# Six held float32 runs per head pair on TensorE, and PSUM banks filled with scores before their first read, in a two-layer attention and mLSTM kernel

## The chip, the cores and the metric

The kernel runs on one core of one Trainium2 chip. The metric is the device time of one execution in microseconds; of several executions the median counts. A profiled execution gives the trace: of each instruction its engine, start and length, and of the TensorE clock the granted share.

The engines are named as in the profile: PE is TensorE (PEld its weight loads), DVE is VectorE, ACT is ScalarE, POOL is GpSimd, SP is SyncE, which issues the weight transfers here. Each engine works off its own list of instructions in order and waits at an instruction until what it needs has been signalled.

## The reference

A sequence of 512 tokens of width 1024, all in float32, runs through two layers: dilated attention with a SwiGLU network, then an mLSTM mixer with a SwiGLU network, and a last norm. The change lies in the attention mixer:

```python
def dilated_attention_mixer(xn, positions, w_in, w_out):
    proj = (xn @ w_in).reshape(B, S, N_GROUPS, 3, ATTN_HEADS, ATTN_HEAD_DIM)   # 3 groups; q, k, v; 8 heads of 128
    for g, (window, dilation) in enumerate(((128, 1), (512, 4), (2048, 16))):
        q = apply_partial_rope(proj[:, :, g, 0], positions) * scale
        k = apply_partial_rope(proj[:, :, g, 1], positions)
        v = proj[:, :, g, 2]
        o, lse = dilated_window_attention(q, k, v, window, dilation)  # banded softmax attention in blocks of 128
        outs.append(o); lses.append(lse)
    wts = softmax(stack(lses), axis=0)              # the three groups are weighed by their log-sum-exp
    return einsum('gbsh,gbshd->bshd', wts, stack(outs)).reshape(B, S, ATTN_WIDTH) @ w_out
```

Its result is added to the input (h = h + mixer), and the first SwiGLU network follows.

## The kernel before

**Projections.** All large products are made in a split form: a float32 matrix is cut into a high and a low part in the type fp32r, and three of the four products of parts are added up (`SPLITS`, three matmuls for each 128 rows). `project` (matmuls in `multiply`, L206) makes one q, one k or group 0's v for two heads: 128 columns of weights stand in the array, the 512 tokens stream through, so its matmuls are 512 wide. `project_tokens` (L237) makes v of groups 1 and 2 with tokens as rows, in matmuls 256 wide. Each is worked off in two weight chunks of 512 rows; a chunk comes by one DMA on SP, ACT makes its high part (L175) and DVE its low part (L176). A chunk has 24 matmuls for each of two PSUM banks. These banks carry the tag "acc", of which there are three.

**Head pairs.** `attention_pair(pr)` runs four times, for two heads each (tiles a0... to a3...). It projects q and k of group 0, 1 and 2 (a1g0q, a1g0k, a1g1q ...), then v of the three groups. Beside these the attention itself is computed in plain float32 matmuls, which the trace shows as two passes each (a transpose as one):

- `scores(g, i, q, k)`: for head i of the pair the scores of a group. Group 0 has two banks with one matmul 128 and three 256 wide (L446), groups 1 and 2 one bank each with four matmuls 128 wide (L459). Behind each matmul DVE reads its part of the bank, adds the mask and takes the row's maximum in one instruction (L448, L460).
- `exponentials(o, i)`: DVE makes the bias `nb`, ACT the exponentials and their sums (L473, L479).
- `turn(i)`: v of group 0, projected with tokens as columns, is transposed (vT, L248) and copied by ACT (L604).
- `weigh()`: group 0 holds its tokens in another order than groups 1 and 2, so their maxima and sums change places by a matmul with a permutation (`exchange`, twice, xps, L492). DVE then makes the coefficients, with an Exp on ACT (L511), and scales the exponentials (L522, L525).
- `transposes(i)`: 15 blocks of exponentials of one head are transposed into four banks (pT, L248), which ACT copies out (pTs, L535).
- `values(i)`: 15 matmuls of these with v add up one head's output (L547, L552), which ACT copies to `o_heads` (oT, L554).

**Order.** The program's text is an order of its own: after each weight chunk `advance()` moves a tick forward and runs the steps that `defer(n, fn)` has put n ticks ahead. `S_AT` and `JOIN_AT` hold these distances. Tile's scheduler then places the instructions of each engine, beginning with those that are ready first by its own account; it may move matmuls of a step in between the projection's matmuls. PSUM has eight banks: three "acc", two "s" (scores, vT, pT), two "o" (values) and one "t" (exchange and small sums).

After the last pair `run_deferred()` runs what is left, the eight heads are split for the output projection (ao tiles, L190 and L191), and `out_project` multiplies with `attn_w_out` (awo0 to awo3). Norm, SwiGLU (f0j, fo), mLSTM and the second SwiGLU follow.

Of the kernel before, what the change touches and what calls it, by code (L numbers as in the profile page):

```python
# [11 lines left out]
F32 = mybir.dt.float32  # L12
# [22 lines left out]
PT_BUFS = 4  # L35
S_AT = ((2, 2), (2, 2), (2, 2))
JOIN_AT = ((5, 6, 7, 7, 8), (4, 6, 6, 6, 7))
STACK_AT = (9, 11, 14, 16)
# [32 lines left out]
def tile_hybrid_dilated_attn_mlstm(  # L71
# [67 lines left out]
    def run_deferred(due=lambda t: True):  # L139
        while True:  # L140
# [4 lines left out]
            ready[0][2]()  # L145

    def acc_tile(name):
        return ps.tile([P, 512], F32, tag="acc", name=name, bufs=3)
# [62 lines left out]
    def project(pairs, w2d, c0, nk, evac, name, hook=None, ready=()):  # L211

        acc = [acc_tile("%s_%d" % (name, m)) for m in range(2)]
        for ch in range((nk + 3) // 4):
            n = min(4, nk - 4 * ch)
            whl = ready[ch] if ready else split_chunk(weight_chunk(w2d, ch, c0, n, "%s_k%d" % (name, ch)))
            for m in range(2):
                multiply(acc[m], whl, pairs, ch, m, nk)
                if 4 * ch + n == nk and hook is None:
                    evac(m, acc[m])  # L220
            if 4 * ch + n == nk and hook is not None:
                hook()
                for m in range(2):
                    evac(m, acc[m])
            advance()

    def project_tokens(pairs, w2d, c0, evac, name, tok=lambda t, tb: t[:, tb * P:(tb + 1) * P]):

        acc = [acc_tile("%s_%d" % (name, m)) for m in range(2)]
        for ch in range(KC // 4):  # L230
            whl = split_chunk(weight_chunk(w2d, ch, c0, 4, "%s_k%d" % (name, ch)))
            for m in range(2):
                for i in range(2):
                    for k in range(4):
                        kk = ch * 4 + k
# [52 lines left out]
    with ExitStack() as actx:  # L288
# [138 lines left out]
        def attention_pair(pr):  # L427
# [7 lines left out]

            def scores(g, i, q, k):
                if g == 0:
                    p0[i] = ap.tile([P, 7, P], F32, tag="p0", name="%sp0_%d" % (nm, i), bufs=2)
                    for b2 in range(2):
                        sp = ps.tile([P, 512], F32, tag="s", name="%ss0" % nm, bufs=2)  # L440
                        o = 0
                        for b in (2 * b2, 2 * b2 + 1):
                            lo_ = max(b - 1, 0) * P
                            w = (b + 1) * P - lo_
                            pb = max(2 * b - 1, 0)
                            nc.tensor.matmul(sp[:, o:o + w], q[:, i, b * P:(b + 1) * P],  # L446
                                             k[:, i, lo_:lo_ + w], start=True, stop=True)
                            nc.vector.tensor_tensor_reduce(  # L448
                                p0[i][:, pb:pb + w // P, :].rearrange("p a b -> p (a b)"),
                                sp[:, o:o + w], mask_band[:, 2 * P - w:], 1.0, -3e38,  # L450
                                op0=ALU.add, op1=ALU.max, accum_out=own[:, 0, 0, i, b:b + 1])
                            o += w
                else:
                    if g == 1:
                        p12[i] = ap.tile([P, 8, P], F32, tag="p12", name="%sp12_%d" % (nm, i), bufs=2)
                    sp = ps.tile([P, 512], F32, tag="s", name="%ss%d" % (nm, g), bufs=2)
                    for c in range(4):
                        sl = slice(c * P, (c + 1) * P)
                        nc.tensor.matmul(sp[:, sl], q[:, i, sl], k[:, i, sl], start=True, stop=True)  # L459
                        nc.vector.tensor_tensor_reduce(  # L460
                            p12[i][:, 4 * (g - 1) + c, :], sp[:, sl], mask_causal if g == 1 else mask_dil,
                            1.0, -3e38, op0=ALU.add, op1=ALU.max, accum_out=mx[:, g - 1, i, c:c + 1])

# [18 lines left out]

            def exchange(o):

                ex = ap.tile([P, 2, 2, 4, 4], F32, tag="ex", name=nm + "ex", bufs=2)
                for st in range(2):
                    nc.vector.tensor_tensor(
                        ex[:, st].rearrange("p i b c -> p (i b) c"),
                        own[:, st, o].rearrange("p i b -> p (i b)").unsqueeze(2).to_broadcast([P, 8, 4]),
                        mask_part.unsqueeze(1).to_broadcast([P, 8, 4]), op=ALU.mult)  # L490
                xps = ps.tile([P, 512], F32, tag="t", name=nm + "xps", bufs=1)
                nc.tensor.matmul(xps[:, :64], perm, ex.rearrange("p s i b c -> p (s i b c)"), start=True, stop=True)  # L492
                ex2 = ap.tile([P, 4, 4, 4], F32, tag="ex2", name=nm + "ex2", bufs=2)
                nc.vector.tensor_tensor(
                    ex2, xps[:, :64].rearrange("p (s b c) -> p s c b", b=4, c=4),
                    mask_part.unsqueeze(1).unsqueeze(1).to_broadcast([P, 4, 4, 4]), op=ALU.mult)
                nc.vector.tensor_reduce(
                    oth[:, :, 1 - o], ex2.rearrange("p (s i) c b -> p s i c b", s=2), axis=AX.X, op=ALU.add)

            def weigh():  # L500

                exchange(0)
                exchange(1)
                cf = ap.tile([P, 16], F32, tag="cf", name=nm + "cf", bufs=2)
# [13 lines left out]
                for i in range(2):  # L518
# [4 lines left out]
                    for c in range(4):  # L523
                        blk = p12[i].rearrange("p (g c) k -> p c g k", g=2)[:, c]
                        nc.vector.tensor_scalar(blk, blk, cf4[:, 1, i, c:c + 1], None, op0=ALU.mult)  # L525

            def transposes(i):
                pts[i] = []
                for src, n0, n1 in ((p0[i], 0, 4), (p0[i], 4, 7), (p12[i], 0, 4), (p12[i], 4, 8)):
                    tp = ps.tile([P, 512], F32, tag="s", name=nm + "pT", bufs=2)  # L530
                    for j in range(n0, n1):
# [6 lines left out]
            def values(i):  # L538
                pt = pts[i]
                hs = slice(i * P, (i + 1) * P)  # L540
                op = ps.tile([P, 512], F32, tag="o", name=nm + "o", bufs=2)
                first = True
# [11 lines left out]
                nc.scalar.activation(o_heads[2 * pr + i], op, AF.Copy)  # L554

            for g in range(3):
                base = g * 3 * D + pr * 256
                qk = []
                for part in range(2):
                    t = tok_tile("%sg%d_%s" % (nm, g, "qk"[part]))  # L560
# [13 lines left out]
                    qk.append(t)  # L574
                for i in range(2):
                    at = S_AT[g][i]
                    defer(at, lambda g=g, i=i, qk=qk: scores(g, i, *qk))
                    if g != 1:
                        defer(at, lambda g=g, i=i: exponentials(g // 2, i))
            steps = (weigh, lambda: transposes(0), lambda: values(0), lambda: transposes(1), lambda: values(1))  # L580
            for at, fn in zip(JOIN_AT[pr == HEADS // 2 - 1], steps):
                defer(at, fn)
            for g in range(3):
# [8 lines left out]
                if g == 0:  # L592

                    vf = ap.tile([P, 2, SEQ], F32, tag="vf", name=nm + "vf")

                    def evac_f(m, acc, vf=vf):
                        nc.scalar.activation(in_order(vf[:, m]), by_block(acc), AF.Copy)

                    def turn(i, v=v, vf=vf):
                        tp = ps.tile([P, 512], F32, tag="s", name=nm + "vT", bufs=2)  # L600
                        for b in range(TB):
                            transpose_into(tp, b, vf[:, i, b * P:(b + 1) * P])
                        for b in range(TB):
                            nc.scalar.activation(v[:, b, i * P:(i + 1) * P], tp[:, b * P:(b + 1) * P], AF.Copy,  # L604
                                                 scale=rnat[:, b:b + 1])
                    project(pair, w_in, 2 * D + pr * 256, KC, evac_f, nm + "g0v")
                    for i in range(2):
                        defer(1, lambda i=i: turn(i))
                else:
                    project_tokens(pair, w_in, g * 3 * D + 2 * D + pr * 256, evac_v, "%sg%dv" % (nm, g))  # L610
# [4 lines left out]
        for k in range(HEADS - 2):  # L615
            split_act(pair[0][k], pair[1][k], o_heads[k], None)
        run_deferred()
        for k in range(HEADS - 2, HEADS):
            split_act(pair[0][k], pair[1][k], o_heads[k], None)

    def add_to_h(c):
        def evac(m, acc):
            nc.vector.tensor_tensor(h[2 * c + m], acc, h[2 * c + m], op=ALU.add)
        return evac

    def out_project(pairs, w2d, nk, name):
        for c in range(KC // 2):
            project(pairs, w2d, c * 256, nk, add_to_h(c), "%s%d" % (name, c))

    out_project(pair, attn_w_out[0], KC, "awo")  # L630

# [456 lines left out]
```

## Time and profile before

| What | Value |
|---|---|
| Runs | 1488.49, 1486.65, 1488.44 us; median 1488.44 |
| Profiled execution | 1486.96 us; its span 1485.2 us |
| Granted TensorE clock, mean | 0.999 |
| Attention pairs, first scores of one to first scores of the next | 47.67, 165.95, 284.25, 402.54 us: 118.3 us each |
| End of the last pair's values | 489.21 us |
| ACT and DVE busy in 166 to 284 us | 40.24 and 65.30 us of 118 |

The span reaches from the first to the last instruction of the engines; 1.76 us of the profiled execution lie around it. The ends of matmuls in the trace are modelled, and matmuls overlap in the pipe, so the distance from one start to the next says more than a record's length.

### The profile page before, as it was taken

The page shows a single profiled execution, that of the slowest core. Times are in us where ns is not written, and L with a number is a line of the kernel's source. Part 1 is how long each engine was busy: PE and PEld are TensorE (multiplying, and loading weights), DVE is VectorE, ACT ScalarE, POOL GpSimd, SP SyncE. Part 2 cuts the span into 40 slices and gives each one's busy share as a digit, 9 for nine tenths or more (in the row PEclk, how much of TensorE's full clock was granted, in tenths as well). Part 3 has the DMA queues.
Part 4 walks back from the last instruction along what each step waited for, and adds up shares of the span by engine and source line. Part 5 has one row for each costly group of instructions (what it writes and reads, how often), then busy time and mean ns, then how long its engine had stood idle before and what let it go on. Part 6 is the DMA issues. An engine that isn't in the chain of part 4 may idle for free. (4 is left out here: it accounts for less than half of the span.)

```text
span 1485.2 us, 18912 instructions
## 1 busy us (share of the span) xinstructions
PE 1468.7 (99%) x7492; PEld 1250.2 (84%) x7492; DVE 768.8 (52%) x1519; ACT 545.6 (37%) x997; POOL 102.8 (7%) x94
## 2 busy tenths in 40 slices
PE   7999999999999999999999999999999999999998
PEld 6889889889889888888888889798888888888887
DVE  7744653664565364444343338987755443443233
ACT  5343225225226342232232223785543332233223
POOL 1000000000000001110110000000000111110011
PEclk9999999999999999999999999999999999999999
DMA  6322222232232223333322333231232333323231
GB/s 191 100 72 86 85 86 71 72 100 78 65 96 71 82 94 100 100 89 97 99 93 93 106 92 87 59 100 58 67 118 87 98 99 100 99 88 98 85 99 72
DMA packets 127529, 134.71 MB, mean 91 GB/s; under 512 B 5392, under 2 KB 119376, under 8 KB 127440
## 3 DMA queue, kind: packets, MB, share of 16 engines
q1 hardware_dynamic: 125328, 131.55, 28.9%
q10 hardware_dynamic: 1808, 1.38, 0.3%
q8 instruction: 59, 0.97, 0.3%
q0 software_dynamic: 304, 0.56, 0.1%
q14 instruction: 30, 0.25, 0.1%
HBM read 131.38 MB, written 2.10 MB: 90 GB/s over the span
## 5 line engine op out<-in xcount | busy, mean ns | idle before, releaser
L206 PE MATMUL f1j<-n_h,f1j_h 128*128 128x512 f32 x352 | 137.1, 389 | 0.0
L206 PE MATMUL f0j<-n_h,f0j_h 128*128 128x512 f32 x352 | 137.1, 389 | 0.0
L206 PE MATMUL f0j<-n_h,f0j_l 128*128 128x512 f32 x352 | 137.0, 389 | 0.0
L206 PE MATMUL f1j<-n_h,f1j_l 128*128 128x512 f32 x352 | 137.0, 389 | 0.0
L206 PE MATMUL f0j<-n_l,f0j_h 128*128 128x512 f32 x352 | 136.9, 389 | 0.0
L206 PE MATMUL f1j<-n_l,f1j_h 128*128 128x512 f32 x352 | 136.9, 389 | 0.0
L176 DVE TENSOR_TENSOR f1j_l<-f1j_w,f1j_h 128x1024 fp32r<-128x1024 f32 x44 | 54.9, 1247 | 54.5 <-ACT f1j_h L175 54.5
L176 DVE TENSOR_TENSOR f0j_l<-f0j_w,f0j_h 128x1024 fp32r<-128x1024 f32 x44 | 54.8, 1245 | 54.5 <-ACT f0j_h L175 54.5
L206 PEld LDWEIGHTS f0j<-n_h,f0j_l 128*128 128x128 f32 x352 | 66.1, 188 | 13.9
L206 PEld LDWEIGHTS f1j<-n_l,f1j_h 128*128 128x128 f32 x352 | 66.1, 188 | 13.8
L206 PEld LDWEIGHTS f1j<-n_h,f1j_h 128*128 128x128 f32 x352 | 66.1, 188 | 13.7
L206 PEld LDWEIGHTS f0j<-n_h,f0j_h 128*128 128x128 f32 x352 | 66.1, 188 | 13.7
L206 PEld LDWEIGHTS f1j<-n_h,f1j_l 128*128 128x128 f32 x352 | 66.1, 188 | 13.6
L206 PEld LDWEIGHTS f0j<-n_l,f0j_h 128*128 128x128 f32 x352 | 66.1, 188 | 13.5
L175 ACT ACTIVATE f0j_h<-f0j_w 128x1024 fp32r<-128x1024 f32 x44 | 46.5, 1057 | 73.3 <-PE f0j L206 72.2
L175 ACT ACTIVATE f1j_h<-f1j_w 128x1024 fp32r<-128x1024 f32 x44 | 46.5, 1057 | 73.3 <-PE f1j L206 72.2
L1020 PE MATMUL fin<-fw_h,f1ah 128*128 128x512 f32 (+1 forms) x198 | 72.8, 368 | 0.0
L1020 PE MATMUL fin<-fw_l,f1ah 128*128 128x512 f32 (+1 forms) x198 | 72.5, 366 | 0.0
L1020 PE MATMUL fin<-fw_h,f1al 128*128 128x512 f32 (+1 forms) x198 | 72.4, 366 | 0.0
L206 PE MATMUL fo<-f0ah,fo_k_h 128*128 128x512 f32 x176 | 68.5, 389 | 0.0
L206 PE MATMUL fo<-f0al,fo_k_h 128*128 128x512 f32 x176 | 68.5, 389 | 0.0
L206 PE MATMUL fo<-f0ah,fo_k_l 128*128 128x512 f32 x176 | 68.5, 389 | 0.0
(1160 smaller groups left out, 3601.2 us busy)
## 6 DMA issues: line engine op xcount, KB each, us to landing
f0j_w<-in_ffn_w_in_dram SPq DMA_DIRECT2D x44, 512.0 KB, 3.5
f1j_w<-in_ffn_w_in_dram SPq DMA_DIRECT2D x44, 512.0 KB, 3.6
fw_w<-in_ffn_w_out_dram SPq DMA_DIRECT2D x22, 512.0 KB, 3.8
fo_k_w<-in_ffn_w_out_dram SPq DMA_DIRECT2D x20, 512.0 KB, 3.5
awo_k_w<-in_attn_w_out_dram SPq DMA_DIRECT2D x8, 512.0 KB, 3.5
mv_k_w<-in_mlstm_w_in_dram SPq DMA_DIRECT2D x8, 512.0 KB, 3.7
mqk_k_w<-in_mlstm_w_in_dram SPq DMA_DIRECT2D x8, 512.0 KB, 3.7
mo_k_w<-in_mlstm_w_in_dram SPq DMA_DIRECT2D x8, 512.0 KB, 3.7
```

Of the source, the lines that this page charges most:

```text
L175: nc.scalar.activation(hi[:, :n], raw[:, :n], AF.Copy)
L176: nc.vector.tensor_tensor(lo[:, :n], raw[:, :n], hi[:, :n].bitcast(F32), op=ALU.subtract)
L206: nc.tensor.matmul(acc, whl[a][:, k, m * P:(m + 1) * P], pairs[b][kk], start=(kk == 0 and (a, b) == SPLITS[0]), stop=(kk == nk - 1 and (a, ...
L1020: nc.tensor.matmul(acc[i][:, cs], a[a_][kk][:, tb * P:(tb + 1) * P], whl[b_][:, k, cs], start=(kk == 0 and (a_, b_) == SPLITS[0]), stop=(k ...
```

## The change

The float32 steps are gathered. `run(*fns)` traces its steps behind the matmul that was last traced before (`tc.issue_after`), and puts an edge from each of its matmuls to its last one; `fenced()` lets the projections' matmuls that are traced later stand behind that last one. The edges give order on TensorE and no signals.

- All scores of group 0 of both heads are one run (`scores0`), all of groups 1 and 2 another (`scores12`). Within a bank all matmuls are traced first, and the reads by DVE after them. The scores of one head go to the two "s" banks, those of the other to the two "o" banks (`score_bank`).
- `scores12` comes three chunks after the last k projection. Before, group 1's scores came two chunks after its k and group 2's two chunks after its k.
- The two exchanges become one, of 128 columns instead of twice 64, and share a run with the transposes of v (`turn`, now for both heads).
- `transposes(0)` is a run, `values(0)` with `transposes(1)` another, `values(1)` the last. The four banks of `transposes` are now two "s" and two "o"; `values` goes to "t".
- In the last pair the runs come at `LAST_AT`; `values(1)` and the splits of the last two heads fall after the first weight chunk of awo0.

Tile names stay; lines move by some 25 to 50. In the order of the changed program TensorE has per pair six groups of float32 matmuls: scores0 between g1q and g1k, scores12 between the two chunks of g1v, exchange and vT between the two chunks of g2v, transposes(0) behind g2v, values(0) with transposes(1) after the first chunk of the next pair's g0q, values(1) after its second chunk. In the last pair all but the first come earlier: scores12 ahead of g1v, exchange and vT ahead of g2v, transposes(0) between g2v's chunks, values(0) with transposes(1) behind g2v, values(1) after the first chunk of awo0. Before the first attention scores and behind the output projection the orders of all engines are those of before, and on SP and POOL they are the same throughout. On ACT the exponentials of groups 1 and 2 now stand ahead of the copies of g1v out of PSUM.

```diff
-S_AT = ((2, 2), (2, 2), (2, 2))
-JOIN_AT = ((5, 6, 7, 7, 8), (4, 6, 6, 6, 7))
+RUN_AT = (2, 3, 5, 6, 7, 8)
+LAST_AT = (2, 4, 5, 6, 7)
...
+    def run(*fns):
+        n0 = len(nc.cur_bb.bb.instructions)
+        with tc.issue_after(last_on_pe()):
+            for fn in fns:
+                fn()
+        end = last_on_pe()
+        for ins in nc.cur_bb.bb.instructions[n0:]:
+            if ins.engine == end.engine and ins is not end:
+                tc.add_manual_dep(end, ins.name, mybir.DependencyInfo(
+                    mybir.DependencyClass.NoSync, mybir.DependencyReason.DATA), reason="run")
+        fence[0] = end
+
+    def fenced():
+        return tc.issue_after(fence[0]) if fence[0] is not None else nullcontext()
...
-                multiply(acc[m], whl, pairs, ch, m, nk)
+                with fenced():
+                    multiply(acc[m], whl, pairs, ch, m, nk)
...
-            def scores(g, i, q, k):
...
-                    sp = ps.tile([P, 512], F32, tag="s", name="%ss%d" % (nm, g), bufs=2)
-                    for c in range(4):
-                        sl = slice(c * P, (c + 1) * P)
-                        nc.tensor.matmul(sp[:, sl], q[:, i, sl], k[:, i, sl], start=True, stop=True)
-                        nc.vector.tensor_tensor_reduce(
...
+            def score_bank(i, name):
+                return ps.tile([P, 512], F32, tag="so"[i], name=name, bufs=2)
...
+            def scores12(qk1, qk2):
+
+                for i in range(2):
+                    p12[i] = ap.tile([P, 8, P], F32, tag="p12", name="%sp12_%d" % (nm, i), bufs=2)
+                    for g, (q, k) in ((1, qk1), (2, qk2)):
+                        sp = score_bank(i, "%ss%d" % (nm, g))
+                        for c in range(4):
+                            sl = slice(c * P, (c + 1) * P)
+                            nc.tensor.matmul(sp[:, sl], q[:, i, sl], k[:, i, sl], start=True, stop=True)
+                        for c in range(4):
+                            sl = slice(c * P, (c + 1) * P)
+                            nc.vector.tensor_tensor_reduce(
...
+                    exponentials(1, i)
...
             def weigh():
 
-                exchange(0)
-                exchange(1)
+                exchange()
...
-                op = ps.tile([P, 512], F32, tag="o", name=nm + "o", bufs=2)
+                op = ps.tile([P, 512], F32, tag="t", name=nm + "o", bufs=1)
...
+                if g == 0:
+                    defer(RUN_AT[0], lambda: run(lambda: scores0(*qks[0])))
+            later_runs = (
+                (lambda: scores12(*qks[1:]),), (weigh, turn),
+                (lambda: transposes(0),), (lambda: values(0), lambda: transposes(1)), (lambda: values(1),))
+            for at, fns in zip(RUN_AT[1:] if pr < HEADS // 2 - 1 else LAST_AT, later_runs):
+                defer(at, lambda fns=fns: run(*fns))
...
-        run_deferred()
-        for k in range(HEADS - 2, HEADS):
-            split_act(pair[0][k], pair[1][k], o_heads[k], None)
...
+        defer(1, last_heads)
+        out_project(pair, attn_w_out[0], KC, "awo", end=1)
+        assert not later
+    out_project(pair, attn_w_out[0], KC, "awo", first=1)
```

## The prediction

> **What bounds the kernel now.** I read the page first, for who is busy. (Columns: engine, busy us, share of the span, instructions; below, busy tenths and granted clock in 40 slices.)
>
> ```profile
> PE 1468.7 (99%) x7492; PEld 1250.2 (84%) x7492; DVE 768.8 (52%) x1519; ACT 545.6 (37%) x997; POOL 102.8 (7%) x94
> PE   7999999999999999999999999999999999999998
> PEclk9999999999999999999999999999999999999999
> ```
>
> TensorE has no gap and its clock is full, so only its own stream can move the time. But a matmul's record is longer than its share of the pipe (389 ns for a 512-wide one that follows the last after 227), so a wait under 0.2 us hides between overlapping records and "99%" can't tell loss from work. I therefore went to the stages of head pair 1, cut where its f32 groups begin, and then to the timeline of TensorE, reading distances between starts. Stages (from:to, length, then busy us and instructions of PE, PEld, DVE, ACT, POOL, clock, DMA):
>
> ```profile
> 165.95:190.91 24.96, 24.96 (x114) 20.67 (x112) 17.55 (x40) 8.08 (x21) 0.00 (x0) 1.00 0.28 85
> 190.91:214.59 23.68, 23.68 (x113) 19.73 (x112) 14.97 (x33) 4.84 (x6) 0.00 (x0) 1.00 0.29 89
> 214.59:234.91 20.32, 20.32 (x169) 20.04 (x168) 6.75 (x27) 13.15 (x48) 0.00 (x0) 1.00 0.22 63
> 234.91:241.16 6.25, 6.25 (x54) 6.25 (x53) 5.07 (x21) 2.13 (x4) 0.00 (x0) 1.00 0.41 135
> 241.16:284.25 43.09, 43.09 (x237) 36.78 (x235) 20.96 (x37) 12.12 (x19) 0.00 (x0) 1.00 0.25 74
> 479.40:484.30 4.90, 4.90 (x45) 4.90 (x45) 1.94 (x2) 2.67 (x5) 0.00 (x0) 1.00 0.50 154
> ```
>
> The first five add to 118.30 us, one pair's period. The sixth is a stretch of f32 passes alone, wanted below. Now two switches between the split projections (L206, L237) and f32 scores (L459):
>
> ```profile
> 72.40 0.39 PE L206 MATMUL a0g2q<-xa_h,a0g2q_k_l 128*128 128x512 f32 x1
> 72.63 0.60 PE L459 MATMUL a0s<-a0g_k,a0g_q 128*128 128x128 f32 x4
> 72.99 0.48 PE L206 MATMUL a0g2k<-xa_h,a0g2k_k_h 128*128 128x512 f32 x1
> 73.30 0.40 PE L206 MATMUL a0g2k<-xa_l,a0g2k_k_h 128*128 128x512 f32 x1
> ...
> 96.67 0.36 PE L237 MATMUL a0g1v<-a0g1v_k_h,xa_h 128*128 128x256 f32 x1
> 96.87 0.28 PE L237 MATMUL a0g1v<-a0g1v_k_l,xa_h 128*128 128x256 f32 x1
> 97.08 0.49 PE L459 MATMUL a0s<-a0g_k,a0g_q 128*128 128x128 f32 x2
> 97.33 0.36 PE L237 MATMUL a0g1v<-a0g1v_k_h,xa_l 128*128 128x256 f32 x1
> 97.53 0.38 PE L459 MATMUL a0s<-a0g_k,a0g_q 128*128 128x128 f32 x2
> ```
>
> The first switch is cheap: four f32 passes (two matmuls; each f32 matmul is two passes, a transpose one) take 0.36 us instead of 4 x 0.11, and the projection matmul behind them 0.31 instead of 0.227; net some 0.03 us. The second is dear: at 96.87 a 256-wide matmul holds the pipe 0.21 us instead of 0.12, and two passes take 0.25 instead of 0.22. This is a score matmul waiting until VectorE has read its bank: in the kernel before, the second and later matmuls of a bank each stand behind such a read.
>
> **The change, part by part.** The price of one pair is its period less what its passes take when nothing waits. Clean paces, start to start: 0.2267 us (512 wide, 10.88 per 48), 0.120 (256 wide, 5.76 per 48), f32 128 wide 0.1105 in scores, 0.1095 in transposes, 0.1117 in values, f32 256 wide 0.2155.
>
> Scores of group 0 stage: 96 x 0.2267 + 4 x 0.109 + 12 x 0.2155 = 24.78 against 24.96: lost 0.18. Group 1 stage: 96 x 0.2267 + 16 x 0.1105 = 23.53 against 23.68: 0.15. Group 2 and vT: 144 x 0.120 + 16 x 0.1105 + 8 x 0.1095 = 19.93 against 20.32: 0.39. Exchange: 48 x 0.120 + 0.34 (its own four passes) = 6.10 against 6.25: 0.15. Transposes, values and the next pair's projections: 144 x 0.2267 + 30 x 0.1095 + 60 x 0.1117 = 42.63 against 43.09: 0.46. Together 1.33 us per pair, over some 23 f32 groups.
>
> Now the edits. *Six held runs:* 17 groups go. Six stay; the four ahead of 512-wide matmuls cost 0.027 each as at 72.63, the two ahead of 256-wide ones about nothing (eight vT passes and the 48 matmuls behind take 6.62 to 6.63 at 222.53, the paces give 6.64): 0.09. *Bank-wise scores:* the reads no longer stand between a bank's matmuls, part of the 1.33. *One exchange instead of two:* two passes at about 0.11 for four that took 0.34: 0.12 saved; on VectorE one product of 128 columns for two of 64, about nothing, off the path. *Fences* on later projection matmuls add order on TensorE and no work. Per pair 1.33 - 0.09 + 0.12 = 1.36; the last pair's groups run into awo and show the same row lengths; four pairs give 5.4 us. No step that moves issues a DMA, and SP's and POOL's orders stay as they were.
>
> What costs nothing only under cover is the waiting at run heads: TensorE now stops with everything behind it. I walk the queues of pairs 0 to 2 with the rows of before, zero at the end of g2k.
>
> *scores12, now one run, a chunk later than group 2's scores were.* g0v ends at 10.88, g1v's first chunk at 16.64, the run's four banks at 17.5, 18.4, 19.3 and 20.2. VectorE reads a 128-wide score every 0.215 us, so head 0 is reduced at 19.4 and, one or two reads of head 1 later, its bias is there at 20.1. ScalarE's exponentials:
>
> ```profile
> 219.51 0.40 ACT L479 ACTIVATE a1p<-a1p,a1nb 128x128 f32<-128x128 f32 x1 [3.40 <-DVE a1nb L468]
> ...
> 225.69 1.62 ACT L604 ACTIVATE a1v<-a1vT,rnat 128x128 f32<-128x128 f32 x6
> ```
>
> Sixteen take 6.18 us, 0.386 each with the read of its sum beneath the next, so from 20.1 they end at 26.3 (head 1's bias, behind a 1.23 us weight split, is there at 22.5, before its turn at 23.2). Queued behind them in ScalarE's order is the copy that frees g1v's first "acc" bank: two rows at 0.36 pace, out at 27.1. TensorE needs that bank for g2v's second half at 20.2 + 5.76 + 2.88 = 28.8. Cover: 1.7 us, the thinnest of these pairs. (scores0 keeps its place behind g1q and waits for the same q and k.)
>
> *Exchange and turn.* TensorE arrives at 31.7, the sums stand at 26.7. *Transposes(0)* start at 38.5. Behind the exchange VectorE has 0.9 us of small operations, a split that waits for ScalarE's of the same chunk (to 34.2), 0.3 us, the Exp of L511 behind six vT copies (to 34.7), 1.0 us up to the scaling, as from 238.32 to 239.33 in the trace, and eight scalings at 0.262: 37.9. Covered, and the last four columns are wanted only 1 us into the run. *Values* come 5.4 us after transposes whose four copies take 2.0. *Last pair:* there scores12 stands before g1v and the exchange at 25.9, sums at 22. The tail: in the trace the last values matmul ends at 489.21 and the copy of oT7 with its two splits at 491.48, 2.27 later; awo_0's second chunk wants that low part after ten matmuls, 2.27 and 0.09 for the first. Just covered; if not, 1 us is the bound, the length of the splits.
>
> **The rivals.** *The banks of g1v come free late* (ends slower). The two score groups share one clump: 16 reductions, then 16 exponentials, and only then the copy. If they go at the sum of their rows, not at their pace (reductions 0.281 + 0.077, exponentials 0.388 + 0.187), the clump grows by 2.3 + 3.0 = 5.3 us, less 1.7 of cover makes 3.6, times three pairs 10.8: 5.4 slower, 1493.8. It costs from 1.7 us of delay and eats the gain at 3.5. For it: the read of g1v's bank really stands behind the exponentials. Against: back-to-back rows of both kinds show the pace. 0.08, three quarters of it slower.
>
> *The waits move to the run heads.* The 0.46 of the transposes stage includes ScalarE freeing "s" banks, and that of the scores VectorE; if runs wait as long at their head, only group 2's 0.39, the exchange and a little come back: some 0.6 per pair, 2.4 in all, 1486.0; with the tail's 1 us 1487.0. Four banks per run speak against it. 0.08.
>
> *The clock drops in long f32 runs.* At the start 16 transposes take 3.59 us, 0.21 each, and later 0.11: half clock for the first 3.3 us of work. A drop like that costs half of 3.3 us; two such runs per pair would cost 8 x 1.65 = 13, against 5.4 gained: 1496. The sixth stage row speaks against it: 45 f32 passes, 15 of them transposes, in 4.90 us at clock 1.00, as long as the longest new run (values(0) and transposes(1), 5.0). 0.03. The Trainium skill (TensorE: Matmul & The Clock Gate, Part 4) says that transposes do not count as TensorE-busy for the clock, a rule against this change; by it alone the rival would hold, while that row, transposes among f32 matmuls, does not show it.
>
> *The change doesn't do what it says:* ordering edges without effect, matmuls placed as before. The changed program's order shows six groups per pair; what is left is that the cost sits elsewhere than in the switches: no difference, 0.03.
>
> **How the numbers follow.** The profiled execution took 1486.96 with a span of 1485.2; less 5.4 that is 1481.6 and 1479.8. The median of the runs is 1488.44 (1486.65 to 1488.49), so 1483.0 (0.78). Its own range is 1481.0 (5.4 below the fastest run, and a little) to 1485; to take in the moved waits it reaches 1486.5. About 0.2%, 3.0 us, is what a measurement of this kernel can tell from no change: faster means under 1485.5. Faster 0.78 + 0.02 of the moved waits = 0.80; same 0.06 + 0.02 (banks a little late) + 0.03 = 0.11; slower 0.06 + 0.03 = 0.09.
>
> **What would show it.** Right: a pair's period of 116.9 us instead of 118.3; f32 runs of x16, x32, x10, x15, x45 and x30 passes (twelve of the first sixteen are 256 wide) at the clean paces; the first g2v matmul of the second bank 0.12 behind the one before. Wrong: a gap of over 0.3 us there, named after ScalarE's copy; a gap before the first pT; a stop at awo_0's second chunk; a granted clock below 1.00 between 42 and 489.

## The result, and the profile after

The median of six runs is 1481.88 us (1481.7 to 1483.5); six runs of the kernel before beside them gave 1487.50 (1486.64 to 1488.49). The ratio is 0.9961, with a 95% interval of 0.9951 to 0.9972: 0.39% faster. The profiled execution took 1481.93 us with a span of 1479.8, against 1486.96 and 1485.2.

The page of the changed kernel, busy times and clock:

```profile
PE 1463.7 (99%) x7484; PEld 1250.0 (84%) x7484; DVE 766.5 (52%) x1507; ACT 545.2 (37%) x997; POOL 102.7 (7%) x94
PE   7999999999999999999999999999999999999998
PEclk9999999999999999999999999999999999999999
```

As before, the page says "99%" and shows no gap: TensorE's busy time shrank by 5.0 us with the span, because the records overlap: a matmul that starts late still starts before the record ahead of it has ended. The same five stages of head pair 1, cut at the same events (from:to, length, then busy us and instructions of PE, PEld, DVE, ACT, POOL, clock, DMA):

```profile
164.58:189.43 24.85, 24.85 (x114) 20.74 (x112) 17.27 (x38) 8.08 (x21) 0.00 (x0) 1.00 0.28 85
189.43:211.19 21.76, 21.76 (x98) 18.02 (x96) 13.36 (x17) 4.84 (x6) 0.00 (x0) 1.00 0.31 97
211.19:232.03 20.84, 20.84 (x178) 20.84 (x176) 8.21 (x43) 11.24 (x40) 0.00 (x0) 1.00 0.19 55
232.03:238.88 6.85, 6.85 (x61) 6.85 (x59) 5.89 (x24) 4.10 (x12) 0.00 (x0) 1.00 0.44 143
238.88:281.55 42.67, 42.67 (x236) 37.01 (x235) 19.96 (x33) 12.01 (x19) 0.00 (x0) 1.00 0.25 75
```

The period is now 116.97 us (three pairs agree to 0.01) against 118.29 on the mean of three, and the float32 runs are those named, of x16, x32, x10, x15, x45 and x30 passes. The second stage holds no scores any more and runs at the clean pace to the digit, 96 x 0.2267 = 21.76; the third takes 20.84 where the paces give 144 x 0.120 + 32 x 0.1105 = 20.82. The switch that was dear before, between 256-wide projections and scores, and the queues behind it (timeline; start, length, engine, line):

```profile
216.82 0.28 PE L261 MATMUL a1g1v<-a1g1v_k_h,xa_l 128*128 128x256 f32 x1
216.94 3.74 PE L494 MATMUL a1s<-a1g_k,a1g_q 128*128 128x128 f32 x32
220.43 0.36 PE L261 MATMUL a1g1v<-a1g1v_k_h,xa_h 128*128 128x256 f32 x1
...
220.52 0.40 ACT L517 ACTIVATE a1p<-a1p,a1nb 128x128 f32<-128x128 f32 x1 [2.32 <-DVE a1nb L506]
...
226.70 1.54 ACT L638 ACTIVATE a1v<-a1g1v,xr 128x256 f32<-128x256 f32 x4
...
237.05 1.14 DVE L563 TENSOR_SCALAR a1p<-a1p,a1cf 128x256 f32<-128x256 f32 x4
```

All 32 score passes start within 3.49 us, 0.109 each. (No record of TensorE between 42 and 489 us names a wait, but neither does one of the kernel before.) The other rows are the cover that the prediction walked; they are read below.

### The profile page after: what moved, and what is told of

Same layout as the page of the kernel before. It is cut to its first block, busy times and chain, and to the rows that moved or that the text cites. A ratio compares the mean times of both kernels' runs of the same rounds, so it can differ in the third digit from the quotient of the medians.

```text
span 1479.8 us, 18900 instructions
## 1 busy us (share of the span) xinstructions
PE 1463.7 (99%) x7484; PEld 1250.0 (84%) x7484; DVE 766.5 (52%) x1507; ACT 545.2 (37%) x997; POOL 102.7 (7%) x94
## 3 DMA queue, kind: packets, MB, share of 16 engines
q1 hardware_dynamic: 125328, 131.55, 28.8%
```

## The experiments

Each kernel was timed beside the kernel before on the same chip (medians of before 1487.4 to 1487.5). Runs of one kernel differ by up to 2.5 us, and pair 0 alone starts at 47.4 to 48.0 us in some of the profiles and at 48.8 to 49.1 in four others (banks_only, two_exchanges, more_runs, exchange_at_once). In these four the first projection matmuls still follow each other in 0.43 us instead of 0.23 until some 15 us; this stretch lies ahead of all scores, and a kernel's parts are not judged by it. So small effects are read from the period, the distance from one pair's first score to the next pair's in the profile, a mean of three; the three agree to 0.02 us where the clock stays full.

| Kernel | Period, us | Median, us | Ratio to before (95%) |
|---|---|---|---|
| before | 118.29 | 1487.50 | |
| after | 116.97 | 1481.88 | 0.9961 (0.9951 to 0.9972) |
| banks_only | 117.67 | 1484.54 | 0.9980 (0.9969 to 0.9990) |
| merged_exchange_only | 118.03 | 1486.89 | 0.9996 (0.9987 to 1.0005) |
| four_banks_only | 117.88 | 1485.00 | 0.9986 (0.9977 to 0.9996) |
| parts_without_runs | 116.99 | 1482.77 | 0.9968 (0.9956 to 0.9980) |
| reads_between | 121.12 | 1497.95 | 1.0067 (1.0052 to 1.0082) |
| s_banks_only | 118.51 | 1488.83 | 1.0009 (1.0000 to 1.0019) |
| two_exchanges | 117.23 | 1483.08 | 0.9971 (0.9959 to 0.9983) |
| more_runs | 117.09 | 1485.45 | 0.9981 (0.9972 to 0.9990) |
| exchange_at_once | 125.24 | 1517.09 | 1.0198 (1.0180 to 1.0217) |
| exchange_at_once_free | 116.99 | 1482.58 | 0.9968 (0.9956 to 0.9980) |
| scores_later | 117.33 | 1484.42 | 0.9979 (0.9969 to 0.9988) |

One question needed no run. With the ordering edges and fences taken out of the changed kernel (`run` only calls its steps), the program comes out the same: the same instructions in the same order with the same waits on every engine. At these places the edges order nothing that would not stand so anyway. What they do at other places is the last group of runs.

### Parts of the change put into the kernel before

**banks_only** traces the score matmuls of a bank ahead of its reads (here groups 1 and 2; group 0 likewise):

```diff
                     for c in range(4):
                         sl = slice(c * P, (c + 1) * P)
                         nc.tensor.matmul(sp[:, sl], q[:, i, sl], k[:, i, sl], start=True, stop=True)
+                    for c in range(4):
+                        sl = slice(c * P, (c + 1) * P)
                         nc.vector.tensor_tensor_reduce(
```

> The kernel before with one part of the change: within a bank all score matmuls are traced ahead of the first read; the two s banks, the ticks, two exchanges and the order of the rest stay. Its order has for group 0's scores three groups per pair instead of five, one instead of four for group 1, one instead of six for group 2. Theory of the sum (waits for reads and banks, 0.027 us for a switch): a pair loses 0.03 instead of 0.15 at group 1, about nothing instead of 0.39 at group 2 (with vT), 0.1 to 0.18 at group 0 as before since head 1 still waits for head 0's banks: 0.5 us gained per pair, period 117.8, 1485.5 in all. Rival (every switch costs the same, 1.33 us over 17 groups, 0.08 each): ten groups fewer, 0.8 per pair, period 117.5, 1484.3.

The period fell by 0.62 us, to 117.67: between the theory's 117.8 and the rival's 117.5, so this run alone does not decide between them; more_runs, below, does. The f32 groups of the scores went from sixteen to five (x8, x4, x4 for group 0, one of x16 for each of groups 1 and 2), and stage by stage the three score stages gave back 0.09, 0.12 and 0.40 us:

```profile
166.73:191.60 24.87, 24.87 (x113) 20.68 (x112) 17.55 (x40) 8.19 (x21) 0.00 (x0) 1.00 0.27 84
191.60:215.16 23.56, 23.56 (x114) 19.81 (x112) 14.97 (x33) 4.84 (x6) 0.00 (x0) 1.00 0.28 91
215.16:235.08 19.92, 19.92 (x170) 19.92 (x169) 6.45 (x27) 13.26 (x48) 0.00 (x0) 1.00 0.23 73
```

That a score matmul of the kernel before waits for VectorE's read shows in its timeline. The read of the bank's first part ends at 97.02, and the score matmul that the prediction shows at 97.08 starts just behind it:

```profile
96.73 0.29 DVE L460 CUSTOM_DVE_ANT_0 a0p<-a0s,acst 128x128 f32<-128x128 f32 x1 [3.57 <-PE a0s L459]
```

**merged_exchange_only** has the one exchange of 128 columns, in its old place; **four_banks_only** has

```diff
-                for src, n0, n1 in ((p0[i], 0, 4), (p0[i], 4, 7), (p12[i], 0, 4), (p12[i], 4, 8)):
-                    tp = ps.tile([P, 512], F32, tag="s", name=nm + "pT", bufs=2)
+                for b, (src, n0, n1) in enumerate(((p0[i], 0, 4), (p0[i], 4, 7), (p12[i], 0, 4), (p12[i], 4, 8))):
+                    tp = ps.tile([P, 512], F32, tag="so"[b // 2], name=nm + "pT", bufs=2)
...
-                op = ps.tile([P, 512], F32, tag="o", name=nm + "o", bufs=2)
+                op = ps.tile([P, 512], F32, tag="t", name=nm + "o", bufs=1)
```

> The kernel before with one part of the change alone: one exchange matmul of 128 columns per pair instead of two of 64, in the old place. The prediction's term: 0.12 us per pair, period 118.18, total 1487.0. By the start-to-start rows of before (each of the two exchanges also costs the projection matmul behind it 0.08 us, and the second is a group of its own): 0.25 us per pair, period 118.05, total 1486.5. Rival (the exchange is hidden, the gain is all in the score reads): period 118.3, 1487.5.

> The kernel before with another part alone: the four transposes of a head take two s and two o banks, the values the t bank, as in the change; the order of scores, exchange and steps as before. Theory (the transposes wait for ScalarE's copy to free the third bank, and the placement puts two or three projection matmuls there meanwhile): 0.19 us lost in each of two transpose groups comes back, period 117.9, total 1486.0. Upper bound 0.46, the whole loss that the prediction put to this stage: 117.84. Rival (the copies are hidden by the matmuls placed between, and one bank for the values costs a wait instead): period 118.3 or more, 1487.5 to 1489.

The exchange alone gave 0.26 us per pair, the transposes' banks 0.41; each single ratio is near the limit of what the times can tell, the periods are not. What the banks do is plain in the timeline of TensorE, with ScalarE's first copies. The kernel before:

```profile
241.16 0.93 PE L248 MATMUL a1pT<-cst,a1p 128*128 128x128 f32 x7
241.85 0.48 PE L206 MATMUL a2g0q<-xa_h,a2g0q_k_h 128*128 128x512 f32 x1
242.09 0.98 ACT L535 ACTIVATE a1pTs<-a1pT 128x512 f32<-128x512 f32 x2
242.16 0.40 PE L206 MATMUL a2g0q<-xa_l,a2g0q_k_h 128*128 128x512 f32 x1
242.40 0.40 PE L206 MATMUL a2g0q<-xa_h,a2g0q_k_l 128*128 128x512 f32 x1
242.74 1.09 PE L248 MATMUL a1pT<-cst,a1p 128*128 128x128 f32 x8
```

and with four banks:

```profile
240.54 1.80 PE L248 MATMUL a1pT<-cst,a1p 128*128 128x128 f32 x15
242.10 0.48 PE L206 MATMUL a2g0q<-xa_h,a2g0q_k_h 128*128 128x512 f32 x1
```

Before, seven transposes fill two banks, the next one needs a bank that ScalarE has yet to copy out, and three projection matmuls stand in the meantime. They hide most of the wait, not all of it: the stretch from the first pT to the end of the second group takes 2.43 us, of which 3 x 0.2267 is projection; the remaining 1.75 stand against 1.56 for fifteen in a row.

**parts_without_runs** has these three parts together, and nothing else of the change: every step at its old place, no runs, no edges.

> The kernel before with three parts of the change together (within a bank the score matmuls ahead of its reads; one exchange; four banks for the transposes), but with the old places for every step: no runs, no edges, the scores of the groups at three places, the turn apart from the exchange. Theory (the parts add, and gathering into six runs is worth some 0.02 us for each group saved, three or four of them): 118.30 - 0.63 - 0.25 - 0.38 = 117.04, total 1482.4. Rival (gathering into runs is itself a large part, as the wording of the change has it, at least 0.3 us per pair): period 117.3 or more, total 1483.2 or more.

The period is 116.99 us, 0.02 from the whole change; the parts add (0.62 + 0.26 + 0.41 = 1.29 of 1.30). Its stages:

```profile
164.86:189.72 24.86, 24.86 (x114) 20.69 (x113) 17.25 (x38) 8.20 (x21) 0.00 (x0) 1.00 0.26 85
189.72:213.28 23.56, 23.56 (x114) 19.81 (x113) 14.97 (x33) 4.84 (x6) 0.00 (x0) 1.00 0.28 90
213.28:233.19 19.91, 19.91 (x169) 19.91 (x168) 6.52 (x27) 13.26 (x48) 0.00 (x0) 1.00 0.24 74
233.19:239.17 5.98, 5.98 (x52) 5.98 (x51) 5.01 (x20) 2.13 (x4) 0.00 (x0) 1.00 0.35 109
239.17:281.84 42.67, 42.67 (x236) 37.02 (x235) 20.85 (x36) 12.01 (x19) 0.00 (x0) 1.00 0.24 75
```

The last stage equals the one after, 42.67. So the rival, that gathering the work into runs is itself a large part, falls: with ten f32 groups per pair instead of six the period is the same to 0.02 us.

### Parts taken out of the changed kernel

**reads_between** puts each score's read right behind its matmul again, with the four banks and the run kept:

```diff
                             nc.tensor.matmul(sp[:, sl], q[:, i, sl], k[:, i, sl], start=True, stop=True)
-                        for c in range(4):
-                            sl = slice(c * P, (c + 1) * P)
                             nc.vector.tensor_tensor_reduce(
```

> The changed kernel, but each score's read is traced right behind its matmul again; four banks, runs and the rest as changed. Theory of the sum as put on record (the reads between a bank's matmuls are part of the 1.33): a score matmul waits again for the read of its bank, now with TensorE held: 0.3 to 0.7 us more per pair, 1.2 to 2.8 in all, 1483 to 1484.7. Rival (four banks in turn leave time for the read: a round of four 128-wide matmuls takes 0.88, a read with its way there and back about 0.7): at most 0.1 per pair, 1482.0.

Both expectations were far too low: 1497.95 us, slower than before, and 4.15 us per pair. The run of 32 passes takes 5.83 us instead of 3.49 (timeline; the idle time before an instruction and its releaser stand in brackets):

```profile
347.07 1.22 DVE L199 TENSOR_TENSOR a2g2v_k_l<-a2g2v_k_w,a2g2v_k_h 128x1024 fp32r<-128x1024 f32 x1
347.13 0.49 PE L492 MATMUL a2s<-a2g_k,a2g_q 128*128 128x128 f32 x2 [0.68 <-DVE a2mx L493]
...
348.20 0.28 DVE L493 CUSTOM_DVE_ANT_0 a2p<-a2s,acst 128x128 f32<-128x128 f32 x1
...
348.55 0.30 PEld L492 LDWEIGHTS a2s<-a2g_k,a2g_q 128*128 128x128 f32 x2 [1.12 <-DVE a2mx L493]
348.55 0.49 PE L492 MATMUL a2s<-a2g_k,a2g_q 128*128 128x128 f32 x2 [0.93 <-DVE a2mx L493]
```

The read that the last matmul awaits (348.20) stands on VectorE behind a weight split of 1.22 us. In the kernel before, the same kind of wait was partly filled with projection matmuls; in a held run nothing may fill it. Besides, the clock fell to half for 3.41 us behind this run in pairs 0, 2 and 3, which is told in the last section. The 4.15 us are 2.34 in this run, 0.83 in the run of group 0 (3.68 us instead of 2.85), and 1.0 from the half clock, 1.5 in each of two of the three periods. Both expectations had left out the split and the clock.

**s_banks_only** lets the transposes of the changed kernel use the two s banks twice, and the values the o banks, as before.

> The changed kernel, but the four banks of the transposes are the two s banks twice, and values goes to o again; runs and the rest as changed. Theory of the sum: the third bank of a run waits for ScalarE's copy of the first, 0.8 us in transposes(0) (a copy of g2v stands ahead) and 0.55 in transposes(1): 1.4 per pair, period 118.3, 5.5 in all, 1487.4: the whole gain. Rival (the banks are not what the held transposes need): 0 to 0.2 per pair, 1482 to 1482.7.

1.54 us per pair, close to the 1.4 expected, and more than the whole change had gained. The run of 15 transposes takes 2.43 and 2.20 us instead of 1.56 (timeline):

```profile
240.55 0.93 PE L272 MATMUL a1pT<-cst,a1p 128*128 128x128 f32 x7
...
241.47 0.98 ACT L582 ACTIVATE a1pTs<-a1pT 128x512 f32<-128x512 f32 x2
...
242.13 0.33 PE L272 MATMUL a1pT<-cst,a1p 128*128 128x128 f32 x1 [0.65 <-ACT a1pTs L582]
```

It is the same wait for ScalarE's copy as in the kernel before, now with nothing in it. The four banks, worth 0.41 us where the wait could be filled, are worth 1.54 where it can't.

**two_exchanges** has two exchanges of 64 columns in the run with the turn, instead of one.

> The changed kernel with the exchange of the two heads' sums undone into two matmuls of 64 columns instead of one of 128, each with its own products, still in one run with the turn. On TensorE: exchange, four vT passes, exchange, four vT passes. The prediction's term: 0.12 us per pair lost again, period 117.08, total 1482.4. If the second exchange waits for its own chain on VectorE (a product and a reduction of the first stand ahead of it): up to 0.7 us more per pair, 1485. Rival (the exchange is worth nothing, the gain is all in waits): period 116.96 to 117.0, 1482.

0.26 us per pair, more than the expected 0.12 and far from none: exchange and turn take 1.28 us instead of 1.02, in the order xps, four vT, xps, four vT. Two passes more at the clean pace are 0.22 of it. That is as much as the merged exchange gave in the kernel before.

**more_runs** cuts the runs by halves and heads, with ticks of half a chunk: twelve f32 groups per pair instead of six.

> The changed kernel with more and shorter runs, put between the two banks of a projection chunk as well: scores0 one run for each head, scores12 one for each bank (from two chunks behind the last k instead of three), values of each head in two (in pairs 0 to 2). Six more groups per pair, 24 in all but for the last pair, and no new wait by the walk of the queues. Theory of the sum (0.027 for a switch into 512-wide matmuls, about nothing into 256-wide ones): three of each, 0.05 to 0.1 per pair, period 117.05, 1482.2. Rival (0.08 for each switch): 0.5 per pair, period 117.45, 1483.8.

0.12 us per pair, 0.02 for each group more: a little above the theory's 0.05 to 0.1, and the rival's 0.08 for each switch falls. The median rose by more, 3.6 us, of which the periods explain 0.5. In the profile pair 0 starts 1.3 us later, with the slow start told above, and in the last pair the exchange comes closer behind its scores and waits 1.5 us for its sums (PE L533 at 464.32).

### What the edges do elsewhere

**exchange_at_once** asks for the exchange and the turn at the place of the scores of groups 1 and 2; **exchange_at_once_free** does the same with the edges taken out.

```diff
-RUN_AT = (2, 3, 5, 6, 7, 8)
-LAST_AT = (2, 4, 5, 6, 7)
+RUN_AT = (2, 3, 3, 6, 7, 8)
+LAST_AT = (2, 2, 5, 6, 7)
```

> The changed kernel, ordering edges kept, with the exchange and the turn of v asked for at the same place as the scores of groups 1 and 2 (RUN_AT 2, 3, 3, 6, 7, 8; LAST_AT 2, 2, 5, 6, 7), two chunks earlier than they were. On TensorE seven vT passes, the exchange and the last vT pass then stand right behind the 32 score passes, and the edges hold every later projection matmul behind them. Theory (the edges do nothing while a run's inputs are there, and cost the whole wait when they are not): the exchange needs the softmax sums, which stand 26.7 us after the end of g2k where TensorE arrives after some 21, so it stops 5 to 6 us in each pair: period 116.96 + 5.7 = 122.7, total 1482 + 4 x 5.7 = 1505 (1501 to 1509; a lowered clock behind the stop would add 1.5 us to a pair). Rival (the exponentials go at the sum of their rows, 0.575 us for each instead of 0.386): a stop of 10 to 12 us, 1526.

> The same early place for the exchange and the turn, and run() only calls its steps: no ordering edges, no fences. The placement then puts projection matmuls of group 2's v between the scores and the exchange. Theory: no stop as long as the exchange comes behind the sums, and one or two more f32 groups per pair at 0.02 to 0.12 us: period 117.0 to 117.2, total 1482.0 to 1483.0. Rival (without edges the exchange is still placed ahead of its sums): a stop of 1 to 5 us in each pair, 1486 to 1502.

With the edges the kernel takes 1517.09 us, without them 1482.58. Without, the exchange stands 50 projection matmuls later, behind its sums, and the period is 116.99, as expected. With them, TensorE stops (windows, then the timeline, of the kernel with edges):

```profile
230.58:237.36 6.78, 0.93 (x10) 0.69 (x8) 3.28 (x19) 6.78 (x35) 0.00 (x0) 0.73 0.25 77
237.36:240.56 3.20, 3.20 (x15) 3.20 (x16) 1.83 (x11) 1.75 (x7) 0.00 (x0) 0.50 0.00 0
```

```profile
236.88 0.16 DVE L519 TENSOR_TENSOR a1own<-a1dn 128x4 f32<-128x4 f32 x1 [2.91 <-ACT a1p L517]
237.08 0.22 DVE L525 TENSOR_TENSOR a1ex<-a1own,cst 128x64 f32<-128x64 f32 x1
...
237.36 0.80 PE L530 MATMUL a1xps<-a1ex,acst 128*128 128x128 f32 x2 [5.85 <-DVE a1ex L525]
```

The seven transposes and the stop take 6.78 us where seven passes are worth 0.77: 6.0 us, forecast 5.7. Of the 7.6 us that pair 1 is longer than after, the other 1.5 are the half clock of the third window (0.37 in the exchange, 1.13 in the projection matmuls behind it); in pair 0 it is 2.8. The total lies above the expected 1501 to 1509 for this half clock, 1.5 to 2.8 us in each pair, and for a longer stop in the last pair, 7.4 us.

**scores_later** puts the scores of groups 1 and 2 one chunk later, with the exchange where it was (RUN_AT 2, 4, 5, 6, 7, 8; LAST_AT 3, 4, 5, 6, 7).

> The changed kernel with the scores of groups 1 and 2 one chunk later (RUN_AT 2, 4, 5, 6, 7, 8; LAST_AT 3, 4, 5, 6, 7), 5.8 us. The exchange then stands where its sums come 32.1 to 32.5 us after the end of g2k by the pace of the walk (exponentials 0.386 us each), and TensorE arrives at 31.7 to 32.5: theory a stop of 0 to 0.4 us per pair, period 117.0 to 117.4, total 1482 to 1484. Rival (exponentials and reductions at the sum of their rows): the sums come 3 to 5 us later, period 120 to 122, total 1494 to 1502. This measures the cover that the walk gave to the exchange.

```profile
233.15 0.16 DVE L519 TENSOR_TENSOR a1own<-a1dn 128x4 f32<-128x4 f32 x1 [2.92 <-ACT a1p L517]
...
233.35 0.22 DVE L525 TENSOR_TENSOR a1ex<-a1own,cst 128x64 f32<-128x64 f32 x1
...
233.63 0.30 PEld L530 LDWEIGHTS a1xps<-a1ex,acst 128*128 128x128 f32 x2 [0.35 <-DVE a1ex L525]
```

The period is 117.33, 0.36 us more, within the theory's 0 to 0.4: the last sum is done at 233.31, 32.4 us after the end of g2k (200.87; expected 32.1 to 32.5), and the exchange's operand at 233.57, 32.7. So the exponentials go at their pace of 0.386 us and not at the sum of their rows.

## Why the prediction was right

The time came within 1.1 us of the forecast (1483.0; the profiled execution 1481.93 for 1481.6, the span 1479.8 for 1479.8). The 1483.0 was counted from the median of three runs of before, 1488.44; from the 1487.50 measured beside the changed kernel the same 5.4 us lead to 1482.1. The prediction's method was to take from the period what its passes cost at clean pace, stage by stage. The runs that each made one part alone allow it to be marked term by term (us per pair):

| Term of the sum | Predicted loss | Given back | By |
|---|---|---|---|
| Group 0 scores | 0.18 | 0.09 | banks_only |
| Group 1 scores | 0.15 | 0.12 | banks_only |
| Group 2 scores and vT | 0.39 | 0.40 | banks_only |
| Exchange, 0.15 and two passes 0.12 | 0.27 | 0.26 | merged_exchange_only |
| Transposes and values | 0.46 | 0.41 | four_banks_only |
| Six runs that stay | -0.09 | | |
| Sum | 1.36 | 1.28; whole change 1.32 | |

What the six runs still cost shows in the changed kernel: its five stages add to 116.97 us, the passes at their paces to 116.85, so 0.12 stayed where 0.09 was put.

**Mis-sized:** group 0's term, by half. In the changed kernel its stage still takes 24.85 us for passes worth 24.78, with the sixteen passes in one run and no wait in the trace. Some 0.04 of these 0.07 stand at the switch behind the run (from 164.58 to 168.55, 3.97 us for 3.93); the rest stays open. The four other terms were right to 0.05.

**Right sum, wrong name:** the text said "17 groups go", as if the groups were the cost. more_runs prices a group at 0.02, so the fourteen that parts_without_runs saves (24 to 10) make some 0.3 of its 1.30, an estimate. The larger rest is waits, for VectorE's reads of score banks and for ScalarE's copies of the transposes, and the second exchange, which is mostly work: two passes at the clean pace are 0.22 of its 0.26. The prediction named both waits itself. Of the exchange it called 0.15 lost and 0.12 saved, because it took the four passes at 0.34 us, in which the pass ahead of a projection shows as 0.03; at the clean pace they are 0.44, and the split is 0.05 and 0.22 with the same sum. Its 0.027 for a switch was near. How it came by that is less sound: in the rows that it shows, the four passes gain as much (0.36 for 0.44) as the matmul behind them loses (0.31 for 0.227), 4 x 0.027 is 0.11 and not 0.09, and the trace of before has 24 groups per pair, of which 18 go, not 23 and 17. So the closeness of the 0.027 is luck; beside the sum of 1.36 these slips are small.

**The fences** "add order and no work": right, and they do not even add order at these places. Against the rival of edges without effect the prediction held the six groups in the changed program's order, as if they were the edges' work. The edges are without effect; the six groups come from the tracing, the banks and the places.

**The walk of the queues**, zero at the end of g2k (200.31 in pair 1 of after), was the step on which the sign hung, and it held to 0.2 us. The first exponential was put at 20.1 and came at 20.2; g1v's first two rows were to be out at 27.1: the copy begins at 226.70, and two rows at 0.36 end it at 227.4, 27.1. TensorE needed that bank at 229.15, 28.8, and the two g2v matmuls there stand 0.12 apart. Head 0's scalings were put at 37.9 and ended at 238.19, 37.9, with the first transposition at 38.57: a cover of 0.7. The sums were put at 26.7 and came at 26.7; the exchange's operand stands at 26.9, and TensorE comes at 31.7:

```profile
226.83 0.16 DVE L519 TENSOR_TENSOR a1own<-a1dn 128x4 f32<-128x4 f32 x1 [2.92 <-ACT a1p L517]
227.03 0.23 DVE L525 TENSOR_TENSOR a1ex<-a1own,cst 128x64 f32<-128x64 f32 x1
```

exchange_at_once, where TensorE does wait for them, has them at the same 26.7.

**The rivals.** *Late g1v banks* would have needed the exponentials at the sum of their rows; the rows of after, exchange_at_once and scores_later show the pace. *Waits at the run heads* did not come: runs stand at 1.556 for 15 transposes, and awo's matmuls behind the last run follow each other in 0.23 to 0.32 us. But the mechanism is real, and s_banks_only is that case: it took the gain and 0.2 more. What kept it away is what the prediction held against it, the four banks. *The clock*: 1.00 from 42 to 489 us; values(0) and transposes(1), 45 passes from 245.97 to 250.88, took 4.91 us (forecast 5.0). The rule of the Trainium skill weighed in the prediction (TensorE: Matmul & The Clock Gate, Part 4), that transposes don't count as TensorE-busy for the clock, is not borne out here. That row alone can't test it, since enough matmuls that are no transposes lie around the fifteen. A window of s_banks_only can (the whole window; the next one; then a3g2v's matmuls in the first, with the columns PE, PEld and ACT alone):

```profile
471.84:475.25 3.41, 2.61 (x24) 2.37 (x23) 3.41 (x6) 3.41 (x8) 0.00 (x0) 1.00 0.03 5
475.25:478.67 3.42, 3.42 (x30) 3.42 (x30) 1.52 (x2) 1.38 (x4) 0.00 (x0) 1.00 0.53 172
471.84:475.25 3.41, 1.00 (x9) 0.88 (x8) 0.00 (x0) 1.00 0.03 5
```

Its first edge lies on that run's grid of clock windows (see the last section): the clock falls at 1482.19, 296 windows later. Fifteen f32 transposes are all of its work but 1.00 us, and the clock stays full, where windows with 1.8 us of work in the last section were followed by half clock. (Two more windows of this run, from 239.74 and 359.21, have 2.76 us of work with 1.15 of it outside the transposes, and stay full too.) So in this kernel f32 transposes keep the clock up. That the clock does drop belongs to stops, not to f32 work (below).

## What to carry to other kernels

Where the busiest engine shows 99%, price its stream by distances between starts against clean paces, stage by stage: here that gave 1.36 us per pair beforehand, and 1.32 came. Look for the gain in what a matmul waits for (who reads the bank first, which bank comes next) rather than in the number of switches, of which one cost 0.02 us. Holding work together by order is safe only where everything it needs stands ready: the same wait of ScalarE cost 0.2 us where other matmuls could fill it and 0.6 to 0.9 where none could, and an exchange asked for too early cost 35 us with the edges and less than 1 without, where the scheduler placed it later.

## What was not expected of the hardware

Stops far shorter than the clock's window halved the clock. In reads_between the half-clock stretches are 3.413 us long and begin at 107.22, 349.57 and 465.62 us; their distances are 71 and 34 times 3.413, so they lie on a fixed grid. TensorE's busy time in the window of the grid just before each, and in one that was not followed by a drop, with the first drop itself:

```profile
103.81:107.22 3.41, 1.81 (x12) 1.43 (x12) 2.79 (x17) 1.79 (x9) 0.00 (x0) 1.00 0.02 7
107.22:110.64 3.42, 3.42 (x18) 3.42 (x17) 0.92 (x6) 3.42 (x19) 0.00 (x0) 0.50 0.50 153
226.69:230.10 3.41, 2.15 (x16) 1.96 (x17) 2.45 (x12) 3.02 (x16) 0.00 (x0) 1.00 0.21 49
346.16:349.57 3.41, 1.80 (x13) 1.43 (x12) 2.79 (x16) 2.37 (x13) 0.00 (x0) 1.00 0.05 10
462.21:465.62 3.41, 1.81 (x14) 1.50 (x13) 2.76 (x17) 2.56 (x13) 0.00 (x0) 1.00 0.11 24
```

The two stops of a run are the same in all four pairs, 0.67 or 0.68 and 0.93 us. In pairs 0, 2 and 3 both fall into one window, TensorE is busy for 1.8 of its 3.41 us, and the next window runs at half clock; in pair 1 a boundary (226.69) cuts through the first stop, the window has 2.15, and the clock stays. By these four windows the same program pays or not by where a boundary falls, and the profile of one pair does not tell what the next will do. A window that is busy throughout at half clock restores the full one: after 107.22:110.64 the clock is back, while in exchange_at_once the first slow windows were busy for 0 to 2.75 us and a second followed, 6.83 us in all. The busy share alone is not the whole rule: in pair 0 of exchange_at_once a window with only 1.62 us of work (104.04 to 107.45) was followed by an empty one at a recorded clock of 1.00, and the drop came one later. In the empty window no matmul ran whose pace could confirm the record. That stays open.

The Trainium skill (TensorE: Matmul & The Clock Gate, Part 1) has a free-running window of 3413 ns; the grid agrees. Its advice to leave no idle gap above about 3 us (same page, Why this matters for your kernels) is too mild by this measurement: two stops of under 1 us were enough.
